# A second quarter-block product in the last map of a decoder layer: product A11·B11 of the second token block made by seven

## The chip, the cores and the metric

The kernel runs on one core of one Trainium2 chip. The metric is the device time of one execution in microseconds (us). Before the change three executions took 1734.28, 1735.79 and 1736.70 us; the median, 1735.79 us, is the time to compare with. A further execution was profiled; every time of a single instruction in this document comes from the profile.

## The reference, cut to what matters

The layer has two sub-layers. The first (an input projection, a gated convolution and a causal pooling, an output projection, a layer norm) is untouched by the change. The second is

```python
h = x * (1.0 + sc2) + sh2                       # x: 2048 tokens x 1024
f = square(relu(h @ w_mlp_in)) @ w_mlp_out      # 1024 -> 4096 -> 1024
x = layer_norm(ALPHA * x + (1.0 + g2) * f, ln2_g, ln2_b)
```

All of it is float32. The change touches `... @ w_mlp_out`, the "second map", for the second half of the tokens.

## The kernel before, in words

**Float32 by three matmuls.** Every operand of a matmul is split (`split`, L87): ScalarE (ACT) casts it to a rounded high part (L88), VectorE (DVE) subtracts that from the value (L89), which gives the low part. `mm3` (L92) multiplies high by high (L93), high by low (L94) and low by high (L95) into one PSUM bank. `tt` (L98) is every plain DVE operation on two tensors, so sums, differences and the adds from PSUM all carry line L98.

**Blocks and products.** The 2048 tokens are worked on in two blocks of 1024 (b = 0, then b = 1). In a block the second sub-layer first runs `up` for eight chunks g of 512 hidden columns, and then `down`, the second map, which multiplies the 1024 x 4096 activations A by the 4096 x 1024 weights B. A and B are cut into half blocks, A11, A12, A21, A22 and likewise B, and the product is made by seven products of half blocks or of sums of them (Winograd's form of Strassen's scheme) in place of eight. `up` makes the activation's sums and stores them in `usum`, and earlier steps made the weights' sums (`w2sum`). In `down` a product is a list of 8 chunks x 4 token tiles x 2 halves of the contraction x 3 matmuls = 192 matmuls of 128x512. `steps` gives the order of the products, each in two steps of four chunks; `table` says for each product which of two sets of four PSUM banks it uses (X or Y), whether it opens them anew, and what becomes of a bank when it is complete (`then`). The output of a block is eight tiles F[0] to F[7] of 128 tokens x 1024. Their left 512 columns are `lo_`, the right ones `hi_`. F[0..3] are the upper tokens and F[4..7] the lower ones. Products 0, 2, 4 and 6 accumulate in one set of banks X one after another; 3 and 5 share Y.

**The quarter product.** In the second block (`b in DEEPER`) product 1, A12·B21, is not made from half blocks: it enters F[0..3][:, lo_] alone, and is made by the same scheme of seven once more, over quarter blocks ("deep"). `closed` (in `up`) writes the quarter sums of A12 in `udeep`, and `sum_deep` (L974), called after some chunks of `up` as `DEEP_SUMS` says, writes those of B21 in `wdeep`. In `down` come eight sets of operands, one per chunk (`deep_operands`: two tiles of 1024 and two of 768 columns, 1.835 MB together, four casts and four subtractions), each followed by `deep_matmuls`: 7 products x 2 token tiles x 3 = 42 matmuls of 128x256. The seven products have a PSUM bank each, in the order p1, p6, p2, p7, p5, p3, p4, and stay open over all eight chunks. Then `deep_sums` puts them together in F: p1 by two ACT copies, the rest by fourteen DVE adds of 128x256, with p5 read twice. The loads of the sets hang on one another in a row (`issue_after`), three sets ahead of the matmuls; the first 12 tiles (`DIRECT`) are loaded straight into the place of their low part.

**What sets the order.** SBUF tiles come from pools: `h` (28 tiles, high and low parts), `r` (5) and `w` (6) for loads, `o` (10; eight of them are F during `down`), and eight PSUM banks `ps`. A new tile takes the place that was released first, and waits for its last reader. The instructions of each engine run in a fixed order, which comes from the order in the code and a scheduler. SP's queue issues the loads (r, w), POOL's queue the stores (usum, udeep, wdeep). At the end, `gated_first`, `last_half` and `Close` scale the output by the gate, add the residual and normalise, tile by tile.

Of the kernel before, what the change touches and what calls it, by code (L numbers as in the profile page):

```python
# [13 lines left out]
P = 128  # L14
# [20 lines left out]
DEEP_SUMS = (0,), (1,), (2,), (3,), (4, 5), (6, 7), (), ()  # L35
# [15 lines left out]
def tile_hybrid_layer(ctx: ExitStack, tc: tile.TileContext, opening, xT, x, wada, win,  # L51
# [141 lines left out]
    udeep = tc.dram_tile([NC, P, 3 * Q], F32, name="udeep")  # L193
    wdeep = tc.dram_tile([NC, P, T + 3 * Q], F32, name="wdeep")
# [779 lines left out]
    def sum_deep(g):  # L974
        a, e = t_o(T), t_o(T)
        nc.sync.dma_start(a, w2[g, 2])
# [6 lines left out]
        nc.gpsimd.dma_start(wdeep[g][:, :T], a)  # L983
        nc.gpsimd.dma_start(wdeep[g][:, T:], e[:, : 3 * Q])
# [6 lines left out]
    def up(b, g, B):  # L991
# [27 lines left out]
        save(c11, 0)  # L1019
# [19 lines left out]
        if g == 0:  # L1039
            yield  # L1040
        else:
            product(5, Z, False)
            join(c12, Z)
        s1 = t_o()
# [17 lines left out]
        def closed(s4):  # L1062
# [10 lines left out]
            nc.gpsimd.dma_start(udeep[g], e[:, : 3 * Q])  # L1073
# [42 lines left out]
    def down(b, F, g2, close):  # L1116
# [4 lines left out]
        steps = [(i, hf) for i in ((1, 0) if deeper else (0, 1)) + (2, 3, 5, 4, 6) for hf in range(2)]  # L1121
# [65 lines left out]
        def gated_first(t, ps):  # L1187
            tt(F[t + 4][:, lo_], ps, g2[:, lo_], ALU.mult)
# [19 lines left out]
        def deep_operands(g):  # L1208
            tiles = []
            for t, src, n in ((t_r, usum[g, 1], T), (lambda: t_w(F32), wdeep[g][:, :T], T),  # L1210
                              (t_r, udeep[g], 3 * Q), (lambda: t_w(F32), wdeep[g][:, T:], 3 * Q)):
                if 4 * g + len(tiles) < DIRECT:
# [6 lines left out]
                if 4 * g + len(tiles) >= DIRECT:  # L1219
                    hi, lo = t_h(), t_h()  # L1220
# [8 lines left out]
        def deep_matmuls(banks, gs, tiles, ns):  # L1229
            for n in ns:  # L1230
                (ut, uq), (wt, wq) = DEEP[n]
                if gs[0] == 0:
                    banks.append(t_ps())
                for g in gs:
                    (uh, ul), (wh, wl) = tiles[g][ut], tiles[g][wt]
                    ws_ = slice(wq * Q, wq * Q + Q)
                    for t in range(2):
                        us = slice(uq * Q + t * P, uq * Q + t * P + P)
                        mm3(banks[n][:, t * Q : t * Q + Q], uh[:, us], ul[:, us], wh[:, ws_], wl[:, ws_],
                            g == t == 0, g == NC - 1 and t == 1, True)  # L1240

        def deep_sums(banks):
            p1, p6, p2, p7, p5, p3, p4 = banks
            def both(j, k, x, ps):
                for t in range(2):
                    src = ps[:, t * Q : t * Q + Q]
                    d = F[t + 2 * j][:, QUARTERS[k]]
# [251 lines left out]
```

## Time and profile before

| | |
|---|---|
| median of three runs | 1735.79 us (1734.28 to 1736.70) |
| the profiled execution | 1735.02 us, of which its span is 1733.2 us, so 1.8 us lie outside of it |
| TensorE clock granted in it | 0.999 |
| `up` of the second block ends, the quarter product begins | 1424.06 us |
| the quarter product ends, product 0 begins | 1464.37 us |
| the last instruction ends | 1733.20 us |

How to read it: PE is TensorE, PEld its weight loads, DVE VectorE, ACT ScalarE, SP and POOL the engines whose queues issue transfers. "L95 PE" is a matmul from line 95. A row `1464.37 0.40 PE L93 ...` starts at 1464.37 us in the span and takes 0.40 us until its modelled end; matmuls overlap, so the price of one is the distance from its start to the next one's start. `[2.56 <-PE ps L95]` behind a row says that the engine had been idle for 2.56 us and that a matmul of line 95 released it. A row of the windows gives the stretch, its length, the busy time and count of instructions of PE, PEld, DVE, ACT and POOL, the clock, the busy share of the sixteen DMA engines and the GB/s. The lines themselves stand in the prediction.

### The profile page before, as it was taken

To read this page: it belongs to the slowest core of one execution; us is meant where nothing else is said; L and a number is where in the kernel's file an instruction comes from. 1 tells how busy PE (TensorE), PEld (TensorE's weight loads), DVE (VectorE), ACT (ScalarE), POOL (GpSimd) and SP (SyncE) were. 2 spreads that over 40 slices of the span, in tenths; PEclk is the share of its full clock that TensorE was granted. 3 is DMA by queue.
4 is the path that set the end of the run, shared out by engine and by line. 5 is a ranking of instruction groups with operands and counts; after the bars stand their busy time and mean duration, and the time that the engine had idled before them with its cause. 6 is when DMAs were issued, how large, how long until landed. Compare 5 with 4: busy or idle time off the path is not lost.

```text
span 1733.2 us, 21912 instructions
## 1 busy us (share of the span) xinstructions
PE 1723.5 (99%) x7855; PEld 1435.5 (83%) x7855; DVE 1314.6 (76%) x1726; ACT 868.1 (50%) x1172; POOL 205.8 (12%) x399
## 2 busy tenths in 40 slices
PE   9999999999999999999999999999999999999998
PEld 7888888888888888888888888888888889888887
DVE  8897798877777686669686789687566778665896
ACT  6323368554445554446573344775444567444451
POOL 0222220122322000100000000102111110000000
PEclk9999999999999999999999999999999999999999
DMA  9998877778888998887572366657545589777771
GB/s 387 345 337 319 302 267 269 267 262 325 311 326 319 381 418 332 291 286 284 196 271 76 110 219 219 230 185 282 215 179 222 197 290 418 294 273 249 267 264 50
DMA packets 142685, 465.24 MB, mean 268 GB/s; under 512 B 16488, under 2 KB 17008, under 8 KB 142576
## 3 DMA queue, kind: packets, MB, share of 16 engines
q1 hardware_dynamic: 97920, 303.39, 48.0%
q0 software_dynamic: 44656, 160.46, 24.4%
q8 instruction: 61, 1.00, 0.2%
q14 instruction: 48, 0.39, 0.1%
HBM read 318.55 MB, written 145.23 MB: 268 GB/s over the span
## 4 chain that ended last, share of the span: by engine, by line
PE 95%; DMA 3%; issue 1%; DVE 1%; ACT 0%; SPq 0%; POOL 0%; DVEq 0%; POOLq 0%
PE ps L95 30%; PE ps L93 30%; PE ps L94 30%; PE ps L425 3%; DMA r<-in_w 1%; DMA usum<-o 1%; PE ps L773 1%; DVE o L98 0%; DMA o<-in_w 0%; DMA o<-in_opening 0%; DVE w L89 0%; DVE r L98 0%; ACT w L88 0%; DVE o L1369 0%; SPq L108 0%
## 5 line engine op out<-in xcount | busy, mean ns | idle before, releaser
L95 PE MATMUL ps<-h,w 128*128 128x512 f32 x1312 | 510.2, 389 | 0.4 <-DVE w L89 0.4
L94 PE MATMUL ps<-h,w 128*128 128x512 f32 x1312 | 510.3, 389 | 0.0
L93 PE MATMUL ps<-h,w 128*128 128x512 f32 x1312 | 510.0, 389 | 0.0
L93 PE MATMUL ps<-h,h 128*128 128x512 f32 (+1 forms) x1176 | 444.2, 378 | 0.0
L95 PE MATMUL ps<-h,h 128*128 128x512 f32 (+1 forms) x1176 | 444.1, 378 | 0.0
L94 PE MATMUL ps<-h,h 128*128 128x512 f32 (+1 forms) x1176 | 444.0, 378 | 0.0
L88 ACT CAST h<-r 128x1024 fp32r<-128x1024 f32 (+2 forms) x186 | 187.8, 1014 | 298.0 <-PE ps L94 186.8
L95 PEld LDWEIGHTS ps<-h,w 128*128 128x128 f32 x1312 | 246.3, 188 | 52.1 <-DVE w L89 0.8
L94 PEld LDWEIGHTS ps<-h,w 128*128 128x128 f32 x1312 | 246.3, 188 | 51.5 <-DVE h L89 0.5
L93 PEld LDWEIGHTS ps<-h,w 128*128 128x128 f32 x1312 | 246.0, 188 | 51.3 <-ACT h L88 0.2
L89 DVE TENSOR_TENSOR h<-r,h 128x1024 fp32r<-128x1024 f32 (+2 forms) x186 | 217.3, 1173 | 93.5 <-ACT h L88 93.0
L88 ACT CAST w<-r 128x1024 fp32r<-128x1024 f32 x156 | 164.3, 1053 | 242.6 <-PE ps L94 231.3
L89 DVE TENSOR_TENSOR w<-r,w 128x1024 fp32r<-128x1024 f32 x156 | 190.5, 1222 | 96.3 <-ACT w L88 95.4
L94 PEld LDWEIGHTS ps<-h,h 128*128 128x128 f32 x1176 | 221.3, 188 | 41.1
L95 PEld LDWEIGHTS ps<-h,h 128*128 128x128 f32 x1176 | 221.3, 188 | 40.8
L93 PEld LDWEIGHTS ps<-h,h 128*128 128x128 f32 x1176 | 221.3, 188 | 40.5
L98 DVE TENSOR_TENSOR o<-o,o 128x1024 f32<-128x1024 f32 (+2 forms) x193 | 171.1, 890 | 41.0 <-DMA usum<-o 31.8
L98 DVE TENSOR_TENSOR o<-o,ps 128x512 f32<-128x512 f32 (+1 forms) x175 | 113.7, 658 | 54.3 <-PE ps L95 53.4
L89 DVE TENSOR_TENSOR h<-w,h 128x1024 fp32r<-128x1024 f32 x114 | 137.6, 1207 | 4.3 <-ACT h L88 4.1
L88 ACT CAST h<-w 128x1024 fp32r<-128x1024 f32 x114 | 118.6, 1040 | 12.8 <-DMA w<-wdeep 4.1
L1013 POOL DMA_DIRECT2D usum<-o x111 | 59.4, 535 | 472.3 <-ACT o L1010 195.0
L98 DVE TENSOR_TENSOR r<-r,r 128x1024 f32<-128x1024 f32 x60 | 73.4, 1223 | 21.5 <-DMA r<-in_w 17.5
(160 smaller groups left out, 1243.0 us busy)
## 6 DMA issues: line engine op xcount, KB each, us to landing
usum<-o POOLq DMA_DIRECT2D x111, 512.0 KB, 4.8
r<-usum SPq DMA_DIRECT2D x109, 512.0 KB, 5.5
w<-w2sum SPq DMA_DIRECT2D x64, 512.0 KB, 5.9
r<-in_w SPq DMA_DIRECT2D x60, 512.0 KB, 6.0
w<-in_w SPq DMA_DIRECT2D x40, 512.0 KB, 7.4
o<-in_w SPq DMA_DIRECT2D x72, 256.0 KB, 6.4
w2sum<-o POOLq DMA_DIRECT2D x64, 256.0 KB, 6.7
msum<-o POOLq DMA_DIRECT2D x18, 512.0 KB, 4.9
```

The source lines that it names most:

```text
L88: high = nc.scalar.copy(hi, src)
L89: return high.ins, nc.vector.tensor_tensor(lo, src, hi.bitcast(F32), op=ALU.subtract).ins
L93: nc.tensor.matmul(ps, whi, xhi, start=first, stop=False, skip_group_check=goes_on)
L94: nc.tensor.matmul(ps, whi, xlo, start=False, stop=False, skip_group_check=goes_on)
L95: nc.tensor.matmul(ps, wlo, xhi, start=False, stop=last, skip_group_check=goes_on)
L98: return nc.vector.tensor_tensor(out_, a, b_, op=op)
L425: nc.tensor.matmul(ps[m, h], wt[:, w : w + P], A[k][p // 2][:, hs], start=k == 0 and p == 0, stop=k == KD - 1 and p == 2)
L773: nc.tensor.transpose(ps[:, t * P : t * P + P], R[4 * h + t][:, k * P : k * P + P], ident)
L1013: nc.gpsimd.dma_start(usum[g, i], r)
```

## The change

Product 0, A11·B11, of the second block's second map is made by seven over quarter blocks too. A11·B11 enters all four quarters of the output, so its result, once put together in F[4..7][:, lo_], is added to F[0..3][:, lo_] and copied to F[0..3][:, hi_] and F[4..7][:, hi_]. What was accumulated on top of product 0 in the banks X now starts new banks, and is added to F when complete.

- `udeep` and `wdeep` have a place for each of the two products. `sum_deep` makes the weights' quarter sums of B21 (i = 1) or B11 (i = 0), and runs for both after every chunk of `up`; before, it ran eight times in all, and not after the last two chunks.
- `up` stores A11 in two pieces, makes four quarter sums of it (four DVE adds of 128x256) and stores those.
- `down` runs sixteen sets of operands back to back, eight of A12·B21 and then eight of A11·B11, and `deep_sums` twice. `DIRECT` holds for the first product's sets alone.
- Products 2 and 3 end in DVE adds to F (`add`) where ACT copies (`keep`) stood; `gated_first` takes three DVE operations for each of its four tiles where it took two.

```diff
-DEEP_SUMS = (0,), (1,), (2,), (3,), (4, 5), (6, 7), (), ()
+DEEP_SUMS = tuple(((0, g), (1, g)) for g in range(8))
...
+        if b in DEEPER:
+            e = t_o()
+            a11, a21, a12, a22 = (c11[:, i * Q : i * Q + Q] for i in range(4))
+            q1, q2, q4, q3 = (e[:, i * Q : i * Q + Q] for i in range(4))
+            tt(q1, a21, a22, ALU.add)
+            tt(q2, q1, a11, ALU.subtract)
+            tt(q3, a11, a21, ALU.subtract)
+            tt(q4, a12, q2, ALU.subtract)
+            nc.gpsimd.dma_start(usum[g, 0][:, QUARTERS[1]], q3)
+            nc.gpsimd.dma_start(udeep[0, g], e[:, : 3 * Q])
...
         def gated_first(t, ps):
-            tt(F[t + 4][:, lo_], ps, g2[:, lo_], ALU.mult)
+            add(t + 4, lo_, ps)
+            gate(t + 4, lo_)
             tt(F[t + 4][:, lo_], F[t + 4][:, lo_], rest[6][t], ALU.add)
...
-            2: (X, False, lambda t, ps: keep(t, hi_, ps)),
-            3: (Y, True, lambda t, ps: keep(t + 4, hi_, ps)),
+            2: (X, deeper, lambda t, ps: put(t, hi_, ps)),
+            3: (Y, True, lambda t, ps: put(t + 4, hi_, ps)),
...
+            work = [(i, g) for i in (1, 0) for g in range(NC)]
+            tiles = [deep_operands(*w) for w in work[:3]]
             left.pop()(t_h(F32))
...
+            for n, (i, g) in enumerate(work):
+                if n + 3 < len(work):
+                    tiles.append(deep_operands(*work[n + 3]))
+                if n + 1 == len(work):
+                    ready = operands(4)
+                if g == 0:
+                    banks = []
+                deep_matmuls(banks, g, tiles[n])
+                if g + 1 == NC:
+                    deep_sums(banks, 0 if i else 4)
+
+            for t in range(4):
+                whole = F[t + 4][:, lo_]
+                tt(F[t][:, lo_], F[t][:, lo_], whole, ALU.add)
+                nc.scalar.copy(F[t][:, hi_], whole)
+                nc.scalar.copy(F[t + 4][:, hi_], whole)
...
-        for n, (i, hf) in list(enumerate(steps))[2 if deeper else 0 :]:
+        for n, (i, hf) in list(enumerate(steps))[4 if deeper else 0 :]:
```

In instructions: PE gets 336 matmuls of 128x256 for 192 of 128x512; DVE gets 105 operations more and ACT 18; POOL's queue issues 414 transfers instead of 374, SP's 671 instead of 647.

At the seam between the two quarter products, DVE's rows in the changed kernel, from the first add of the first product's `deep_sums` on (`ps_1823` is the bank of p6, `ps_1824` p2, `ps_1825` p7; `h_1879`, `h_1882`, `h_1885` and `h_1888` are the four low parts of the ninth set, the first of A11·B11, and `h_1891`, `h_1894` belong to the tenth):

```order
L98 TENSOR_TENSOR o_1776_11468<-o_1776_11468,ps_1823_11577 128x256
L89 TENSOR_TENSOR h_1879_11886<-r_1877_11883,h_1878_11885 128x1024
L98 TENSOR_TENSOR o_1777_11469<-o_1777_11469,ps_1823_11577 128x256
L89 TENSOR_TENSOR h_1882_11892<-w_1880_11889,h_1881_11891 128x1024
L89 TENSOR_TENSOR h_1885_11898<-r_1883_11895,h_1884_11897 128x768
L89 TENSOR_TENSOR h_1888_11904<-w_1886_11901,h_1887_11903 128x768
L98 TENSOR_TENSOR o_1776_11468<-o_1776_11468,ps_1824_11584 128x256
L98 TENSOR_TENSOR o_1777_11469<-o_1777_11469,ps_1824_11584 128x256
L98 TENSOR_TENSOR o_1778_11470<-o_1776_11468,ps_1825_11591 128x256
L89 TENSOR_TENSOR h_1891_11952<-r_1889_11949,h_1890_11951 128x1024
L98 TENSOR_TENSOR o_1779_11471<-o_1777_11469,ps_1825_11591 128x256
L89 TENSOR_TENSOR h_1894_11958<-w_1892_11955,h_1893_11957 128x1024
```

DVE in the kernel before, where its one quarter product ends and product 0 begins (`ps_1799` is p6, `ps_1800` p2; the `h` are low parts of product 0's operands):

```order
L89 TENSOR_TENSOR h_1856_11836<-r_1853_11831,h_1855_11835 128x1024
L89 TENSOR_TENSOR h_1858_11840<-w_1854_11833,h_1857_11839 128x1024
L98 TENSOR_TENSOR o_1752_11332<-o_1752_11332,ps_1799_11441 128x256
L98 TENSOR_TENSOR o_1753_11333<-o_1753_11333,ps_1799_11441 128x256
L89 TENSOR_TENSOR h_1862_11848<-r_1859_11843,h_1861_11847 128x1024
L98 TENSOR_TENSOR o_1752_11332<-o_1752_11332,ps_1800_11448 128x256
```

Before, the first two low parts of what follows stood ahead of the adds; in the changed kernel every low part of the ninth set stands behind the first add. The rest of the changed sequence goes on in the same way (p5, then the bank of p3, with the low parts of the eleventh set between):

```order
L98 TENSOR_TENSOR o_1776_11468<-o_1776_11468,ps_1826_11598 128x256
L98 TENSOR_TENSOR o_1777_11469<-o_1777_11469,ps_1826_11598 128x256
L98 TENSOR_TENSOR o_1776_11468<-o_1776_11468,ps_1827_11605 128x256
L89 TENSOR_TENSOR h_1903_12018<-r_1901_12015,h_1902_12017 128x1024
L98 TENSOR_TENSOR o_1777_11469<-o_1777_11469,ps_1827_11605 128x256
L89 TENSOR_TENSOR h_1906_12024<-w_1904_12021,h_1905_12023 128x1024
```

Behind these stand two more low parts, two adds of p4 (`ps_1828`) and the second two of p5 (`ps_1826`). PE's rows in the changed kernel at the point where the second quarter product opens its sixth bank, `ps_1930` (its seven are `ps_1925` to `ps_1931`; a wait on an engine's counter stands in brackets):

```order
L94 MATMUL ps_1929_12149<-h_1894_11958,h_1896_11963 128x256
L95 MATMUL ps_1929_12149<-h_1893_11957,h_1897_11964 128x256
L93 MATMUL ps_1925_12121<-h_1905_12023,h_1902_12017 128x256 [waits Activation_49]
L93 MATMUL ps_1927_12135<-h_1905_12023,h_1902_12017 128x256
L93 MATMUL ps_1930_12156<-h_1881_11891,h_1884_11897 128x256 [waits DVE_49]
L94 MATMUL ps_1930_12156<-h_1882_11892,h_1884_11897 128x256
```

The second product's matmuls do not run set by set: the scheduler has put the ones of the banks that come free late behind those of the tenth set. `ps_1930` opens 62 rows behind the first matmul of the second product, and 64 rows of the sets nine to eleven (126 in all) stand from it on. In the first quarter product's last set, p6's last matmul stands 17 rows ahead of the end and p1's 33 rows ahead; in the kernel before, p6's last stood 30 rows ahead of the end.

78 lines of the change are left out of this document (35 added, 43 removed).

## The prediction

> **What bounds the kernel now.** I read the page's shares and the chain of work first, then the waits of PE.
>
> ```profile
> span 1733.2 us, 21912 instructions
> PE 1723.5 (99%) x7855; PEld 1435.5 (83%) x7855; DVE 1314.6 (76%) x1726; ACT 868.1 (50%) x1172; POOL 205.8 (12%) x399
> PE 95%; DMA 3%; issue 1%; DVE 1%; ACT 0%; SPq 0%; POOL 0%; DVEq 0%; POOLq 0%
> PE ps L127 <- DVE o L129: 1.1, 1, 1.1
> PE ps L425 <- DVE h L396: 0.5, 1, 0.5
> PE ps L95 <- DVE w L89: 0.4, 1, 0.4
> PE ps L127 <- DVE h L200: 0.4, 1, 0.4
> ```
>
> PE is busy for 99% of the span and holds 95% of the chain that ended last. Its waits for other engines come to 2.4 us in the whole run (1.1 + 0.5 + 0.4 + 0.4). So the time is the sum of the matmuls, and a change can win only what it takes from that sum, and lose whatever makes PE wait where it doesn't now. The windows of the second map show how near the other resources stand to that:
>
> ```profile
> 1424.06:1464.37 40.31, 40.31 (x338) 40.31 (x336) 33.30 (x37) 27.63 (x32) 2.67 (x5) 1.00 1.02 408
> 1445.00:1465.00 20.00, 20.00 (x166) 19.91 (x166) 16.52 (x19) 15.07 (x18) 0.00 (x0) 1.00 1.03 418
> 1425.00:1430.00 5.00, 5.00 (x44) 5.00 (x43) 4.75 (x7) 5.00 (x7) 0.69 (x3) 1.00 0.98 352
> 1464.37:1733.20 268.83, 261.62 (x1178) 217.49 (x1176) 193.04 (x237) 111.60 (x149) 4.27 (x8) 1.00 0.66 239
> ```
>
> The quarter product (first row) is the tightest stage of the kernel: PE without a gap for 40.31 us, DVE at 33.30 of 40.31 us (83%), weight loads as long as the stage, and the DMA engines full at 408 GB/s. What follows it (last row) runs at 239 GB/s and DVE at 72%. The change puts a second stage of the tight kind in the place of an easy one.
>
> **What PE saves.** The matmuls are priced by the distance of their starts.
>
> ```profile
> 1464.25 0.28 PE L95 MATMUL ps<-h,h 128*128 128x256 f32 x1
> 1464.37 0.40 PE L93 MATMUL ps<-h,h 128*128 128x512 f32 x1
> 1465.76 0.39 PE L93 MATMUL ps<-h,h 128*128 128x512 f32 x1
> 1467.80 0.39 PE L93 MATMUL ps<-h,h 128*128 128x512 f32 x1
> ```
>
> Nine matmuls of 128x512 lie between 1465.76 and 1467.80: 2.04 / 9 = 0.2267 us each, so product 0 by half blocks is 192 x 0.2267 = 43.5 us. A quarter product is 40.31 us for 336 of 128x256, or 0.120 each. The saving is 43.5 - 40.3 = **3.2 us**, and no other term of the change can make PE faster. The narrow form costs 53% of the wide one and not half, which takes two thirds of what one product in eight would be. The Trainium skill prices them alike: "TensorE: Matmul & The Clock Gate", section "Back-to-back issue gap", gives 262 cycles for 256 columns and 518 for 512; worked out from these as an estimate at its 2.4 GHz, the saving would be 4.8 us, but the trace has 0.120 and 0.2267 us, and its rows decide.
>
> **Up.** Each of the eight chunks gets four DVE adds of 128x256 (0.34 us each by the row of seven below, some 1.4 us), and the weights' sums for one more chunk.
>
> ```profile
> 1355.15 1.23 DVE L98 TENSOR_TENSOR o<-o,o 128x1024 f32<-128x1024 f32 x1 [3.10 <-DMA usum<-o]
> 1370.72 1.23 DVE L89 TENSOR_TENSOR w<-r,w 128x1024 fp32r<-128x1024 f32 x1 [4.22 <-ACT w L88]
> wdeep<-o POOLq DMA_DIRECT2D x8, 512.0 KB, 6.2
> wdeep<-o POOLq DMA_DIRECT2D x8, 384.0 KB, 6.0
> udeep<-o POOLq DMA_DIRECT2D x8, 384.0 KB, 5.7
> ```
>
> These rows lie in the sixth chunk of `up`, which makes two sums of weights already, and DVE idles 3.1 and 4.2 us at single places of it while PE waits for nothing. I cost the DVE work of `up` at 0; that idle time hides it, and without it 1.4 us a chunk would show.
>
> **The start of the quarter product.** The stores are another matter at the last chunk. Both sums of the eighth chunk are now made there, where before the last two chunks made none: 2 x (512 + 384) KB = 1.835 MB more, just ahead of a stage whose DMA engines are full. At 417 to 418 GB/s (the second row of the windows above) that is 4.4 us by which the loads come later. What stands against it is the lead of the sets:
>
> ```profile
> 1445.87 0.96 DVE L89 TENSOR_TENSOR h<-w,h 128x768 fp32r<-128x768 f32 x1
> 1450.54 0.95 DVE L89 TENSOR_TENSOR h<-w,h 128x768 fp32r<-128x768 f32 x1
> ```
>
> These are the last low parts of the sixth and seventh set, ready at 1446.8 and 1451.5. A set takes PE 40.31 / 8 = 5.04 us, so the sixth begins at 1424.06 + 5 x 5.04 = 1449.26, and its second product, the first that reads that part, 0.7 us later at 1450.0. The lead is 3.2 us, and 3.5 for the seventh. A delay of 4.4 us against 3.2 leaves **1.0 us** of stall (1.2, rounded down since some of the stores land ahead of the loads). Its bounds are 0, if all of them do, and 2 us, if DVE's order makes the late loads push its own work back further.
>
> **The seam.** Here the second product's operands meet the first one's `deep_sums`. E is the end of the first product. Its prices:
>
> ```profile
> 1460.25 0.65 ACT L1249 COPY o<-ps 128x256 f32<-128x256 f32 x2 [3.05 <-PE ps L95]
> 1460.78 1.06 ACT L88 CAST h<-r 128x1024 fp32r<-128x1024 f32 x1
> 1461.74 1.05 ACT L88 CAST h<-w 128x1024 fp32r<-128x1024 f32 x1
> 1449.67 0.95 DVE L89 TENSOR_TENSOR h<-r,h 128x768 fp32r<-128x768 f32 x1
> 1461.03 0.75 DVE L98 TENSOR_TENSOR o<-o,ps 128x256 f32<-128x256 f32 x2 [2.56 <-PE ps L95]
> 1461.88 1.23 DVE L89 TENSOR_TENSOR h<-r,h 128x1024 fp32r<-128x1024 f32 x1
> 1463.02 0.41 DVE L98 TENSOR_TENSOR o<-o,ps 128x256 f32<-128x256 f32 x1
> 1470.36 2.40 DVE L98 TENSOR_TENSOR o<-o,ps 128x256 f32<-128x256 f32 x7
> ```
>
> By distances of starts, a low part of 1024 columns is 1.14 us of DVE (1461.88 to 1463.02), one of 768 columns 0.86 (1449.67 to 1450.54, above), an add 0.33 ((2.40 - 0.41) / 6). In the kernel before p6's bank was complete 30 matmuls ahead of the end, at 1464.37 - 3.6 = 1460.77, and the add began 0.26 us later. Now it is complete 17 matmuls ahead, at E - 2.0, so DVE begins at E - 1.8. It then has its rows in the order shown: p6 (two adds), four low parts of the ninth set, p2 (2), p7 (2) and p5 (2) among four low parts of the tenth, p3 (2) among the eleventh's, and at the end p4 and p5. Summed up: the ninth set is ready at E + 2.9, p2's bank free at 3.6, p7's at 5.4, the tenth set at 8.3, p5's first adds at 8.9, p3's bank at 10.7, the eleventh set at 13.6, p4's bank at 14.3, p5's at 14.9. ACT isn't late: its casts at 0.95 us run ahead of all of these.
>
> PE has 126 matmuls in the ninth to eleventh set, 15.1 us. Its first low part comes at E + 1.2, but the waits that it meets one after another overlap, and the last one decides: the sixth bank, opened behind 62 matmuls (at E + 7.4 if nothing held it up), with 64 behind it. Banks are taken in the order of their release, so I take it for p3's, free at 10.7. PE ends the eleventh set at 10.7 + 64 x 0.12 = E + 18.4 instead of 15.1: **3.3 us** of stall. Bounds: if DVE's adds slip in earlier, or the bank is p7's, what is left is the first wait of 1.2 us; if the bank is p5's, read last, 14.9 + 7.7 - 15.1 = 7.5 us. The value taken is that of the order of the adds. What is queued behind PE's waiting matmul is the rest of the three sets, and DVE, which waits for none of it there, goes on.
>
> **The end of the second product.** The low parts of product 2's first operands now stand behind the add of p6 as well; by the same count their weights' part is ready at 1.2 us after the end, of which the first matmuls of 0.2267 us cover some: **0.5 us** (0 to 1.2). The four adds and eight copies that spread the result have until product 2's banks are added, at least a step of 96 matmuls or 21.8 us later, and cost nothing.
>
> **The tail.** Two rows price the four adds more in `gated_first`, and one the adds of product 3.
>
> ```profile
> 1704.68 0.69 DVE L98 TENSOR_TENSOR o<-o,r 128x512 f32<-128x512 f32 x1
> 1709.40 0.69 DVE L98 TENSOR_TENSOR o<-o,ps 128x512 f32<-128x512 f32 x1 [4.02 <-PE ps L95]
> 1593.92 1.23 DVE L98 TENSOR_TENSOR r<-r,o 128x1024 f32<-128x1024 f32 x1 [10.58 <-DMA r<-nsave]
> ```
>
> Four adds of 0.69 us are 2.8 us, and DVE idles 4.0 us behind the last of these operations: 0. Products 2 and 3 now need DVE where ACT did the copies. At product 3's end an add of the last bank can come to stand behind an operation that waits for the residual's load (third row, 10.58 us idle); PE opens that bank again for product 5's last tile, 18 matmuls or 4.1 us later. Bounds 0 and 6.5 us (10.6 - 4.1), taken 0, since a wait of which all lies behind that product's end would need the load to be issued 10 us later than now.
>
> **The sum.** -3.2 + 1.0 + 3.3 + 0.5 = +1.6 us on the profiled execution's 1735.02 us: 1736.6. The median stands 0.8 us over that execution, so the forecast is **1737.5 us**, rounded up.
>
> **Rivals.**
> 1. *The waits are hidden and only the saving shows.* For it: two of the three stalls are 1 us or less, and PE waits nowhere in this stretch now. Against it: at the seam DVE has 14.9 + 1.8 = 16.7 us of work in an unbroken row, and PE must have its middle. Time: 1735.8 - 3.2 = 1732.6.
> 2. *Slower: the sixth bank is p5's.* It is read twice, by DVE's last two adds at E + 14.9. Then the stall at the seam is 7.5 us instead of 3.3 and the time 1737.5 + 4.2 = 1741.7. For it: p5's bank is read first ahead of p3's. Against it: PE's row that opens the sixth bank waits for DVE, and the next wait for DVE, 12 rows on, is for the eleventh set's second low part (E + 11.9), which would need no wait if DVE were already known to be at 14.9. This decides from the place of the bank alone.
> 3. *Slower: the transfers bind at the start.* In the window from 1425 to 1430 they ran at 352 GB/s. If that held from the start of the stage to the sixth set, 25 us, 0.065 x 25 = 1.6 MB would be missing on top of the 1.835 MB, 8 us at 417 to 418 GB/s: less the lead of 3.2, a stall of 4.9 instead of 1.0 us, so 1741.4. Against it: 408 GB/s over the whole stage. The Trainium skill, "DMA: Bandwidth & Descriptors", section "Where 436 GB/s comes from", speaks for this rival: between HBM and SBUF a core's share of the memory, about 358 GB/s, binds. The trace disagrees with that as a limit, with 418 GB/s over 20 us.
> 4. *Slower: product 3's add waits for the residual*: up to 6.5 us, 1744.0; it decides only if DVE reaches that row before the load lands and after product 3 has ended.
>
> **How the numbers follow.** The forecast has 0.52, the first rival 0.13, the second 0.15, the third 0.12, the fourth 0.08. The forecast's own terms reach from -3.2 + 0 + 1.2 + 0 = -2.0 to -3.2 + 2 + 3.3 + 1.2 = +3.3 without the second rival's bank, or 1733.8 to 1739.1, a little more with the runs' own spread of 1.2 us on either side. The range of 8 in 10 is 1732.3 to 1742.5: it takes in the first three rivals. A measurement can tell 0.2% from no change here, 3.5 us; the saving alone is 3.2. So faster by more has 0.04 (part of the first rival); within 0.2%, 1732.3 to 1739.3, are the rest of the first rival (0.09), the forecast without its upper end (0.44) and a little of the fourth (0.03), 0.56 together; slower are the rest of the forecast (0.08) and of the fourth (0.05), the second and the third: 0.40.
>
> **What would show it.** Each quarter product at 0.120 us a matmul, and a list of PE's waits with new rows for DVE's L98 and L89, in the 15 us behind the first product's end, of 3 to 4 us together; about 1 us in the sixth and seventh set for a load; half a microsecond behind the second product. If the seam shows no wait, the first rival holds and my row of DVE is wrong; if it shows 7 us, the bank is p5's. If `up` ends later than 1424 us, its cover was thinner than I took it for. If waits lie behind 1600 us, it is the fourth rival or the tail, which I cost at nothing.

## The result and the profile after

The changed kernel takes 1738.36 us (median of 14 runs, 1737.30 to 1739.48). The kernel before, run beside it, takes 1734.59 us (14 runs, 1734.16 to 1736.70), 1.2 us less than the three runs that the prediction started from. The ratio is 1.0019, with an interval of 1.0011 to 1.0027: slower by 3.8 us. The forecast was 1737.5 us, 1.7 us more than before; of the change it gave less than half, and that the time is only 0.9 us off it is luck in part, since the kernel before took 1.2 us less beside it. The profiled execution took 1738.62 us, and its span grew by 3.6 us, from 1733.2 to 1736.8.

The page's shares, the chain of work, and then the waits of PE in the whole run:

```profile
span 1736.8 us, 22481 instructions
PE 1723.7 (99%) x7999; PEld 1441.0 (83%) x7999; DVE 1360.5 (78%) x1832; ACT 880.2 (51%) x1190; POOL 227.2 (13%) x439
PE 97%; DMA 1%; DVE 1%; issue 1%; ACT 0%; DVEq 0%; SPq 0%; ACTq 0%
```

```profile
PE ps L94 <- DVE h L89: 1.4, 2, 1.0
PE ps L93 <- ACT o L1000: 1.4, 1, 1.4
PE ps L127 <- DVE o L129: 1.1, 1, 1.1
PE ps L93 <- DVE o L98: 1.0, 2, 0.6
PE ps L93 <- ACT h L88: 0.6, 1, 0.6
PE ps L425 <- DVE h L396: 0.2, 1, 0.2
```

The list has four new rows: waits for low parts (L89), for adds (L98), for a cast (L88), and one for an ACT copy of L1000, which is `keep` in `up`. Where they lie shows PE's timeline:

```profile
1180.44 0.50 PE L93 MATMUL ps<-h,w 128*128 128x512 f32 x1 [1.39 <-ACT o L1000]
...
1425.48 0.28 PE L93 MATMUL ps<-h,h 128*128 128x256 f32 x1
...
1451.68 0.50 PE L93 MATMUL ps<-h,h 128*128 128x256 f32 x2 [0.61 <-ACT h L88]
...
1466.91 0.28 PE L93 MATMUL ps<-h,h 128*128 128x256 f32 x1
1468.21 0.39 PE L94 MATMUL ps<-h,h 128*128 128x256 f32 x1 [1.01 <-DVE h L89]
...
1472.40 0.39 PE L93 MATMUL ps<-h,h 128*128 128x256 f32 x1 [0.58 <-DVE o L98]
...
1477.73 0.39 PE L93 MATMUL ps<-h,h 128*128 128x256 f32 x1 [0.47 <-DVE o L98]
...
1510.70 0.86 PE L93 MATMUL ps<-h,h 128*128 128x512 f32 x3
1511.99 0.50 PE L94 MATMUL ps<-h,h 128*128 128x512 f32 x1 [0.43 <-DVE h L89]
...
1729.28 0.28 PE L95 MATMUL ps<-h,h 128*128 128x256 f32 x1
```

The time of each term is the distance between such places, not the idle time in brackets, since the first matmuls behind a wait are slower too. `up` ends at 1425.48 instead of 1424.06: +1.4. (The profile of before has a wait of 0.43 us at 519 us, in the first block, which this one hasn't, so the wait in `up` itself costs somewhat more than 1.4.) The first quarter product takes 1466.91 - 1425.48 = 41.4 us instead of 40.3: +1.1. The second takes 1510.70 - 1466.91 = 43.8 us: +3.5 over 40.3. In the kernel before, product 0 ended by its price at 1464.37 + 43.53 = 1507.90, and the last matmul, at 1725.71, stood 217.8 us behind that; here it stands 1729.28 - 1510.70 = 218.6 us behind the second product: +0.8. Less the saving of 43.5 - 40.3 = 3.2 us, that is 1.4 + 1.1 + 3.5 + 0.8 - 3.2 = 3.6 us, the growth of the span. The windows over both quarter products show 82.47 us of PE work in 85.22, and the transfers at 393 GB/s:

```profile
1425.48:1510.70 85.22, 82.47 (x673) 81.06 (x672) 70.13 (x88) 55.73 (x65) 4.84 (x9) 1.00 1.00 393
```

### The profile page after: what moved, and what is told of

It is laid out like the page before. It is cut to its first block, busy times and chain, and to the rows that moved or that the text cites. A ratio compares the mean times of both kernels' runs of the same rounds, so it can differ in the third digit from the quotient of the medians.

```text
span 1736.8 us, 22481 instructions
## 1 busy us (share of the span) xinstructions
PE 1723.7 (99%) x7999; PEld 1441.0 (83%) x7999; DVE 1360.5 (78%) x1832; ACT 880.2 (51%) x1190; POOL 227.2 (13%) x439
## 4 chain that ended last, share of the span: by engine, by line
PE 97%; DMA 1%; DVE 1%; issue 1%; ACT 0%; DVEq 0%; SPq 0%; ACTq 0%
PE ps L94 31%; PE ps L93 31%; PE ps L95 31%; PE ps L425 3%; PE ps L773 1%; DMA r<-udeep 1%; DMA w<-w2sum 0%; DVE h L89 0%; DVE o L98 0%; PE ps L149 0%; DVE h L200 0%; PE ps L127 0%; ACT h L88 0%; DVE o L1391 0%; DVE o L1397 0%
## 5 line engine op out<-in xcount | busy, mean ns | idle before, releaser
L88 ACT CAST h<-r 128x1024 fp32r<-128x1024 f32 (+1 forms) x194 | 194.4, 1007 | 275.7 <-PE ps L94 150.5
L88 ACT CAST w<-r 128x1024 fp32r<-128x1024 f32 x156 | 164.2, 1053 | 244.8 <-PE ps L94 232.5
L89 DVE TENSOR_TENSOR h<-r,h 128x1024 fp32r<-128x1024 f32 (+1 forms) x194 | 224.3, 1161 | 75.7 <-ACT h L88 75.2
L94 PEld LDWEIGHTS ps<-h,h 128*128 128x128 f32 x1224 | 230.2, 188 | 41.0 <-DVE h L89 2.6
L93 PEld LDWEIGHTS ps<-h,h 128*128 128x128 f32 x1224 | 228.2, 188 | 41.2 <-DVE o L98 1.5
L95 PEld LDWEIGHTS ps<-h,h 128*128 128x128 f32 x1224 | 230.2, 188 | 38.0
L89 DVE TENSOR_TENSOR w<-r,w 128x1024 fp32r<-128x1024 f32 x156 | 190.2, 1220 | 81.2 <-ACT w L88 80.2
L98 DVE TENSOR_TENSOR o<-o,o 128x1024 f32<-128x1024 f32 (+2 forms) x221 | 183.1, 834 | 43.2 <-DMA usum<-o 34.2
L98 DVE TENSOR_TENSOR o<-o,ps 128x512 f32<-128x512 f32 (+1 forms) x197 | 124.1, 640 | 63.4 <-PE ps L95 53.2
L89 DVE TENSOR_TENSOR h<-w,h 128x1024 fp32r<-128x1024 f32 x122 | 144.8, 1187 | 4.1 <-ACT h L88 4.0
L88 ACT CAST h<-w 128x1024 fp32r<-128x1024 f32 x122 | 125.2, 1026 | 16.2 <-DMA w<-wdeep 7.6
L1013 POOL DMA_DIRECT2D usum<-o x103 | 55.1, 535 | 378.0 <-DVE o L98 166.3
L98 DVE TENSOR_TENSOR r<-r,r 128x1024 f32<-128x1024 f32 x60 | 73.3, 1222 | 24.8 <-DMA r<-in_w 20.3
```

Of the source, the lines that this page charges most:

```text
L88: high = nc.scalar.copy(hi, src)
L89: return high.ins, nc.vector.tensor_tensor(lo, src, hi.bitcast(F32), op=ALU.subtract).ins
L93: nc.tensor.matmul(ps, whi, xhi, start=first, stop=False, skip_group_check=goes_on)
L94: nc.tensor.matmul(ps, whi, xlo, start=False, stop=False, skip_group_check=goes_on)
L95: nc.tensor.matmul(ps, wlo, xhi, start=False, stop=last, skip_group_check=goes_on)
L98: return nc.vector.tensor_tensor(out_, a, b_, op=op)
```

## The experiments

All ratios are to the kernel before on the same chip. "Both quarter products" is the distance from the first matmul of 128x256 to the first one behind the second product; without any wait it would be 2 x 40.31 = 80.6 us. It and the end of `up` are read from each run's one profiled execution. Those of up_only and seam_copies took 2.0 and 2.2 us more than their medians, with waits of PE of 0.93 us at 519 us and of 1.78 us at 1400 us, so their `up` ends later than in most executions. Differences of 1 to 2 us between the variants are within the overlap of the intervals; there the distances in the traces are the firmer evidence.

| run | median, us | ratio (interval) | over before, us | `up` ends | both quarter products, us |
|---|---|---|---|---|---|
| changed kernel | 1738.36 | 1.0019 (1.0011 to 1.0027) | +3.8 | 1425.48 | 85.22 |
| up_only | 1737.35 | 1.0017 (1.0008 to 1.0026) | +2.8 | 1426.86 | 41.14 (one) |
| down_only | 1732.20 | 0.9986 (0.9977 to 0.9996) | -2.4 | 1423.26 | 81.02 |
| seam_copies | 1736.49 | 1.0013 (1.0004 to 1.0022) | +1.9 | 1426.94 | 83.88 |
| sums_spread | 1756.26 | 1.0123 (1.0108 to 1.0139) | +21.7 | 1444.54 | 83.62 |
| e_only | 1733.68 | 0.9993 (0.9984 to 1.0002) | -1.1 | 1424.93 | 81.02 |
| w_only | 1737.67 | 1.0015 (1.0006 to 1.0024) | +2.9 | 1425.31 | 84.10 |
| last_no_adds | 1737.43 | 1.0015 (1.0007 to 1.0024) | +2.7 | 1425.22 | 84.20 |
| sums_in_block1 | 1743.10 | 1.0045 (1.0033 to 1.0058) | +8.4 | 1434.07 | 81.03 |
| seam_order | 1737.46 | 1.0018 (1.0009 to 1.0028) | +2.7 | 1425.25 | 84.69 |
| seam_p3_first | 1737.07 | 1.0013 (1.0005 to 1.0022) | +2.4 | 1425.45 | 83.57 |
| best | 1734.85 | 1.0001 (0.9992 to 1.0010) | +0.1 | 1423.74 | 83.78 |
| best_act | 1732.26 | 0.9987 (0.9978 to 0.9996) | -2.4 | 1423.43 | 81.03 |

### up_only: the change's `up` without the second quarter product

The kernel before with the changed kernel's lines in `up` and `sum_deep`; product 0 reads all of `usum[g, 0]`, so A11 is stored whole and q3 goes to a place of its own:

```diff
+            nc.gpsimd.dma_start(qdeep[g], q3)
+            nc.gpsimd.dma_start(udeep[0, g], e[:, : 3 * Q])
```

> The kernel before, with the stage `up` of the changed kernel: all sums for the second quarter product are made and stored, but product 0 stays one of half blocks and reads none of them. My theory (the work of `up` is not hidden): PE waits 1.4 us at the beginning of the second chunk, near 1180 us, and about 1.1 us in the sixth or seventh set of the quarter product, so 2.5 us over the kernel before, and a seam as before. Rival (the wait at 1180 us was an accident of one execution): nothing at 1180 us, at most 1.1 us over the kernel before.

PE's rows at the second chunk and in the sixth set:

```profile
1181.82 0.50 PE L93 MATMUL ps<-h,w 128*128 128x512 f32 x1 [1.39 <-ACT o L1001]
...
1453.03 0.39 PE L93 MATMUL ps<-h,h 128*128 128x256 f32 x1 [0.58 <-ACT h L88]
```

Both are there, the first with the same 1.39 us, and the median grew by 2.8 us: `up` is not hidden. The theory missed one thing. The end of the one quarter product waits as well, 0.43 us for a low part at 1469.29, which the kernel before does not: something in `up` reaches into a later stage.

### down_only: the second map's change with the `up` of before

```diff
-DEEP_SUMS = tuple(((0, g), (1, g)) for g in range(8))
+DEEP_SUMS = ((1, 0),), ((1, 1),), ((1, 2),), ((1, 3),), ((1, 4), (1, 5)), ((1, 6), (1, 7)), (), ()
...
-            for t, src, n in ((t_r, usum[g, i], T), (lambda: t_w(F32), wdeep[i, g][:, :T], T),
+            for t, src, n in ((t_r, usum[g, i], T), (lambda: t_w(F32), wdeep[1, g][:, :T], T),
```

> The changed kernel with the stage `up` of the kernel before: the second quarter product reads the operands of the first once more, so that A11·B11 is replaced by other data of the same size. My theory (three terms of the second map, without the late stores): -3.2 of matmuls, +3.5 at the seam, +0.8 behind the second product, so +1.1 us over the kernel before, with no wait in the first product's sets. Rival (the loads of sixteen sets in a row are too much for the DMA engines by themselves): the wait of about 1.1 us in the sixth or seventh set is still there, +2.2 us.

Expected was +1.1, measured -2.4 us. The windows over both quarter products, with PE's busy time behind the length:

```profile
1423.26:1504.28 81.02, 81.02 (x673) 80.77 (x672) 66.64 (x80) 53.92 (x64) 2.66 (x5) 1.00 0.99 385
```

81.02 us, and PE busy in all of it: the seam costs 0.4 us, not 3.5. The sums of the first product, the operands of the second and PE's matmuls are the same in number as in the changed kernel. So the seam's price isn't that of two quarter products behind one another. It comes from `up`, and the effects don't add: +2.8 and -2.4 make +0.4, and the whole change +3.8.

### seam_copies: the late banks given back early

```diff
+            k, j4 = t_o(), t_o()
+            for d, bank in ((k[:, :H], p5), (k[:, H:], p3), (j4[:, :H], p4)):
+                nc.scalar.copy(d, bank)
+            p5, p3, p4 = k[:, :H], k[:, H:], j4[:, :H]
```

> The changed kernel, but the banks of p5, p3 and p4 are copied to SBUF by ACT as soon as they are complete, and DVE adds from there. My theory (the seam waits for PSUM banks that DVE gives back too late): the last bank is free 5 to 6 us behind the end of the first product instead of 14, and the seam's 3.5 us fall to about 1.5, what the ninth set's low parts cost; 2.0 us under the changed kernel. Rival (DVE's work as a whole is too much at the seam, wherever the banks are): the seam stays at 3 us or more, since no add is saved, and the time is the changed kernel's.

1.9 us under the changed kernel. Both products take 83.9 us, of which 0.8 belong to the wait in the sixth set (0.53 us of idle time there; the second product begins at 1468.04, 41.1 us behind the first), so the seam costs about 2.5 us instead of 3.5. PE's waits that are left at the seam:

```profile
1469.33 0.38 PE L94 MATMUL ps<-h,h 128*128 128x256 f32 x1 [1.01 <-DVE h L89]
...
1473.52 0.39 PE L93 MATMUL ps<-h,h 128*128 128x256 f32 x1 [0.58 <-DVE o L98]
```

The wait at the sixth bank is gone, and the one for the ninth set's first low part is as long as before. PE does wait for banks at the seam, behind something that is late already.

### sums_spread: other chunks for the weights' sums

```diff
-DEEP_SUMS = tuple(((0, g), (1, g)) for g in range(8))
+DEEP_SUMS = (((0, 0),), ((1, 0), (0, 1)), ((1, 1), (0, 2)), ((1, 2), (0, 3), (1, 3)), ((0, 4), (1, 4), (0, 5)), ((1, 5), (0, 6), (1, 6)), ((0, 7), (1, 7)), ())
```

> The changed kernel with the weights' sums in other chunks of `up`: 1, 2, 2, 3, 3, 3, 2 and 0 of them instead of 2 each. My theory (the sums in the first chunk make the wait at 1180 us, those in the last chunk the late loads): both waits go, 2.5 us under the changed kernel. Rival A (the wait at 1180 us comes of the four new adds and their tile, not of the weights' sums): only 1.1 us go. Rival B (three sums in a chunk are too many): new waits in the middle of `up`, no gain.

Rival B, far beyond what it said: 21.7 us slower. In the sixth to eighth chunk PE waits 2.2, 3.6 and 6.0 us for the low parts of `up`'s own weights, and behind each wait it runs at half its clock. The first of them in the windows, right behind the wait (the clock stands behind the five engines):

```profile
1325.77:1327.04 1.27, 1.27 (x6) 1.05 (x6) 1.20 (x4) 0.00 (x0) 0.29 (x2) 1.00 1.01 348
1327.04:1330.41 3.37, 3.37 (x9) 2.63 (x8) 2.25 (x4) 0.00 (x0) 1.39 (x3) 0.50 0.98 325
1330.41:1334.50 4.09, 4.09 (x19) 3.41 (x18) 0.90 (x3) 0.00 (x0) 0.00 (x0) 0.99 1.02 396
```

The wait at 1180 us is still there with one sum after the first chunk, so it isn't a matter of the second sum alone.

### e_only and w_only: the two halves of `up`

e_only keeps A11's quarter sums and has the weights' sums of before; w_only has both weights' sums after every chunk and leaves A11's out. The second product reads the first one's operand for what is missing (lines not shown):

```diff
 e_only:
-DEEP_SUMS = tuple(((0, g), (1, g)) for g in range(8))
+DEEP_SUMS = ((1, 0),), ((1, 1),), ((1, 2),), ((1, 3),), ((1, 4), (1, 5)), ((1, 6), (1, 7)), (), ()
 w_only:
-        if b in DEEPER:
-            e = t_o()
...
-            nc.gpsimd.dma_start(udeep[0, g], e[:, : 3 * Q])
```

> The changed kernel with the weights' sums of the kernel before (B21 alone, none after the last two chunks); A11's quarter sums are made and stored, and the second quarter product multiplies them by B21's sums, so that A11·B11 is replaced by A11·B21. Theory after the first runs (what costs at the start and at the seam is the weights' sums of the last chunks, which set where DVE's low parts of the ninth set stand): no wait in the first product's sets, a seam of 0.4 us as with the stage `up` of before, and only the 1.4 us at 1180 us, since A11's tile in the first chunk puts ACT's copies behind a third cast: 1.0 us under the kernel before. Rival (A11's sums and their stores are enough to bring the waits back): start and seam of 4 us or more in all, 3 us over the kernel before.

> The other half: the changed kernel with both weights' sums after every chunk, but without A11's quarter sums; the second quarter product multiplies the first one's activations by B11's sums, so that A11·B11 is replaced by A12·B11. The same theory: the seam's 3.5 us, the 1.1 us at the start and 0.8 us behind the second product are back, and at 1180 us ACT's copies stand behind a third cast here too, 1.4 us: about the time of the changed kernel, 3 to 4 us over the kernel before. Rival: the weights' sums are hidden, and it stays 2 us under the kernel before.

Both came out as the theory had it: -1.1 us and +2.9 us. e_only has both quarter products in 81.02 us and a single new wait:

```profile
1180.00 0.50 PE L93 MATMUL ps<-h,w 128*128 128x512 f32 x1 [1.39 <-ACT o L1000]
```

w_only has the seam (84.10 us for both products) and the same 1.4 us at the second chunk. So either half is enough for the wait at 1180 us, and the weights' sums alone make the seam. In w_only the sixth set does not wait.

### last_no_adds: the last chunk's bytes without its adds

```diff
-        a, e = t_o(T), t_o(T)
+        a = t_o(T)
...
+        e = t_o(T) if g < NC - 1 else a
...
+        if g == NC - 1:
+            nc.gpsimd.dma_start(wdeep[i, g][:, :T], a)
+            nc.gpsimd.dma_start(wdeep[i, g][:, T:], a[:, : 3 * Q])
+            return
```

> The changed kernel, but after the last chunk the weights are stored as they are, the same number of bytes without the eight adds, so that one eighth of both quarter products' weights is wrong. Theory of the prediction (the bytes of these stores delay the loads): the wait of about 1.1 us in the sixth or seventh set stays, and with it the changed kernel's time. Rival, from the trace (eight adds of 0.34 us stand ahead of the fourth set's low parts on DVE and keep its r and w tiles, and the next loads wait for them): the wait falls to 0.3 us or less; DVE's order at the seam is unchanged and so is its 3.5 us; 1 us under the changed kernel.

0.9 us under the changed kernel, the rival's number, and no wait in the sixth set. As a proof of that wait's cause it is weak: seam_p3_first below, with the changed kernel's `up` and first product untouched, has none either, while the changed kernel, seam_copies and seam_order show 0.61, 0.53 and 0.29 us. The wait comes and goes by small amounts. Firm is what the adds do to the loads. The load of the sixth set's third tile goes out, in the kernel before, in this run and in the changed kernel:

```profile
1432.29 0.32 SPq L1218 DMA_DIRECT2D r<-udeep  x1
```

```profile
1434.40 0.32 SPq L1240 DMA_DIRECT2D r<-udeep  x1
```

```profile
1437.47 0.32 SPq L1235 DMA_DIRECT2D r<-udeep  x1
```

From the beginning of the quarter product (1424.06, 1425.22, 1425.48) that is 8.2, 9.2 and 12.0 us. The eight adds cost 2.8 of the 3.8 us, at the same bytes. They stand on DVE ahead of the low parts of the first sets, whose `r` tiles the next loads need.

Two sets later it is the bytes, not the adds. SP's wait for a store between 1436 and 1456 us, and the load behind it, the first of the eighth set, in the changed kernel, in this run and in e_only:

```profile
SPq L1235 <- DMA usum<-o: 8.6, 1, 8.6
1452.04 0.32 SPq L1235 DMA_DIRECT2D r<-usum  x1
```

```profile
SPq L1240 <- DMA usum<-o: 9.6, 1, 9.6
1451.85 0.32 SPq L1240 DMA_DIRECT2D r<-usum  x1
```

```profile
SPq L1235 <- DMA usum<-o: 3.0, 1, 3.0
1441.71 0.32 SPq L1235 DMA_DIRECT2D r<-usum  x1
```

The load reads the last chunk's part of A12, and POOL's queue has the store of that behind the last chunk's weights' sums. With their bytes and without their adds the wait is as long as in the changed kernel; without the sums (e_only) it is 3.0 us, and the load goes out 10 us earlier. The ninth set's loads follow it in the row, so they are late as well.

### sums_in_block1: six of the weights' sums moved ahead

```diff
-DEEP_SUMS = tuple(((0, g), (1, g)) for g in range(8))
+DEEP_SUMS = ((((1, 0), (0, 0)), ((1, 1),), (), (), (), (), (), ((0, 1), (1, 2), (0, 2))), ((), ((1, 3), (0, 3)), ((1, 4), (0, 4)), ((1, 5), (0, 5)), ((1, 6), (0, 6)), ((1, 7), (0, 7)), (), ()))
...
-            if b in DEEPER:
-                for i, n in DEEP_SUMS[g]:
-                    sum_deep(i, n)
+            for i, n in DEEP_SUMS[b][g]:
+                sum_deep(i, n)
```

> The changed kernel, correct in all its parts, with six of the sixteen weights' sums made in the first block's `up` (2, 1, 0, 0, 0, 0, 0, 3 after its chunks) and ten in the second's (0, 2, 2, 2, 2, 2, 0, 0), none after the first chunk and none after the last two. Theory: none of the waits at 1180 us, at the start and at the seam is left, and the saving shows: 2 to 2.5 us under the kernel before. Rival (the sums cost wherever they are; three sums of the first block's last chunk hold up its own second map): a new wait of 1 to 3 us at the beginning of the first block's second map, and a time between the kernel before and the changed one.

The waits at 1180 us, at the start and at the seam are gone, all three, as the theory said (81.03 us for both products). One new one costs more than all of them; it lies not where the rival had it but behind the first block's first chunk, where two sums were put on top of what is made there:

```profile
340.56 0.80 PE L93 MATMUL ps<-h,w 128*128 128x512 f32 x1 [7.42 <-ACT o L1000]
```

### seam_order: DVE's order pinned

```diff
-                split(r[:, :n], hi[:, :n], lo[:, :n])
+                lows.append(split(r[:, :n], hi[:, :n], lo[:, :n])[1])
...
+            with nullcontext() if t0 else tc.issue_after(lows[4 * NC + 1]):
+                both(0, 1, (0, 0), p6)
```

> The changed kernel with one thing pinned: the first product's adds of p6 may not stand ahead of the low part of the ninth set's second tile, so that DVE has at the seam the order that it has without the weights' sums of the last chunks; no work is taken away. Theory (the seam's 3.5 us are the price of an order, in which the ninth set stands behind the adds and all the later banks behind it): the seam falls to 0.4 to 1 us, and the waits at 1180 us and in the sixth set stay; 2.5 to 3.1 us under the changed kernel. Rival (the ninth set's data come too late, and the order only follows them): DVE waits for them ahead of the adds, PE's banks come later still, and the time is the changed kernel's or more.

Missed; the rival had it. The ninth set's first low parts now stood ahead of the adds, but DVE waited 1.70 us for ACT's cast ahead of the first of them, and the second product, from 1466.11 to 1509.94, took 43.8 us as in the changed kernel. The 0.9 us by which the median fell are what the shorter wait in the sixth set and the missing one behind the second product come to. So the theory that DVE's order makes the seam is wrong as it stood.

### seam_p3_first: p3's adds ahead of p5's

```diff
-            both(0, 1, (0, 1), p5)
             both(0, 1, (0, 1), p3)
+            both(0, 1, (0, 1), p5)
```

> The changed kernel with p3's two adds ahead of p5's first two in the order of the sums. Theory (at the seam PE waits for p3's bank, with half of three sets queued behind it): the bank is free at 8.9 us behind the end of the first product in place of 10.7, PE's rows behind it are 71 in place of 64, and the seam costs 2.3 to 2.5 us in place of 3.5; about 1 us under the changed kernel. Rival (it is p5's bank, as the prediction's second rival had it): it is read later than before, and the seam is not shorter.

Half of it: the two products take 83.57 us, and without a wait in the sixth set that leaves 3.0 us for the seam instead of 3.5. The rest of the 1.3 us in the median is the missing wait of that set. The bank is p3's, but with it earlier the low parts come next and hold PE nearly as long.

### best: the sums where none had cost, and DVE's order pinned

The lines of seam_order, and:

```diff
-DEEP_SUMS = tuple(((0, g), (1, g)) for g in range(8))
+DEEP_SUMS = (((), ((1, 0),), (), (), (), (), (), ((0, 0), (1, 1), (0, 1))), ((), ((1, 2), (0, 2)), ((1, 3), (0, 3)), ((1, 4), (0, 4)), ((1, 5), (0, 5)), ((1, 6), (0, 6)), ((1, 7), (0, 7)), ()))
```

> The changed kernel, correct in all its parts, with the order at the seam pinned as in the run before, and the weights' sums at places where none of the waits arose so far: 0, 1, 0, 0, 0, 0, 0, 3 after the first block's chunks and 0, 2, 2, 2, 2, 2, 2, 0 after the second's. Theory: the saving of 3.2 us less 0.4 at the seam and 0.4 behind the second product, 2.4 us under the kernel before, and no wait of PE behind the first 10 us. Rival (each place that is filled costs its own wait, the sums cost 1 to 3 us wherever they are put): no faster than the kernel before.

The waits in `up` and in the sixth set are gone, the seam of 3.2 us is not, and the time is that of the kernel before. This run shows why. ACT and then DVE ahead of the seam:

```profile
1454.12 0.83 ACT L88 CAST h<-w 128x768 fp32r<-128x768 f32 x1
1459.93 0.65 ACT L1264 COPY o<-ps 128x256 f32<-128x256 f32 x2 [4.98 <-PE ps L95]
1460.46 1.06 ACT L88 CAST h<-r 128x1024 fp32r<-128x1024 f32 x1
```

```profile
1461.56 1.23 DVE L89 TENSOR_TENSOR h<-r,h 128x1024 fp32r<-128x1024 f32 x1 [5.31 <-ACT h L88]
```

ACT idles 4.98 us ahead of the two copies of p1, because p1's bank is complete only then, and the ninth set's first cast stands behind the copies. DVE idles 5.31 us for that cast. In the traces of down_only, e_only and sums_in_block1 the order on ACT is the other one: two casts of the ninth set, then the copies.

### best_act: ACT's copies of p1 behind two casts

best, with one pin more (`parts` holds each cast and its low part):

```diff
+            with nullcontext() if t0 else tc.issue_after(parts[4 * NC + 1][0]):
+                both(0, 0, None, p1)
```

> The last run's kernel with one more thing pinned: ACT's two copies of p1 may not stand ahead of the cast of the ninth set's second tile. The last two runs took the first theory of the seam down: with DVE's rows in the good order the seam still cost 3.1 to 3.2 us, and DVE idled 5.3 us ahead of the ninth set's first low part. New theory: it is ACT's order. The two copies wait for p1's bank, which PE completes 4 us ahead of the end of the first product, and the ninth set's casts stand behind them though their data are there; the low parts, and all that DVE does at the seam, come 4 us late. With the copies behind two casts the seam falls from 3.1 to about 0.4 us, and the time is 2.7 us under the last run's, 2.5 us under the kernel before. Rival (the loads of the ninth set come too late): ACT waits for them where it waited for PE, the seam stays at 2 to 3 us, and the time at the kernel before's.

The seam is gone: 81.03 us for both products, and 2.6 us less than best from the place of two copies of 0.3 us each. ACT at the same place, and all waits of PE in the run:

```profile
1454.79 1.05 ACT L88 CAST h<-r 128x1024 fp32r<-128x1024 f32 x1 [0.38 <-DMA r<-usum]
1456.03 1.05 ACT L88 CAST h<-w 128x1024 fp32r<-128x1024 f32 x1 [0.20 <-DMA w<-wdeep]
1459.63 0.37 ACT L1264 COPY o<-ps 128x256 f32<-128x256 f32 x1 [2.55 <-PE ps L95]
```

```profile
PE ps L127 <- DVE o L129: 1.1, 1, 1.1
PE ps L127 <- DVE h L200: 0.6, 1, 0.6
PE ps L425 <- DVE h L396: 0.2, 1, 0.2
```

No wait is left behind the first 9 us. The second quarter product is then worth 2.4 us (0.9978 to 0.9996): the saving of 3.2 less 0.4 at the seam and 0.4 behind.

## Why the prediction was right, and where it was not

**The bound and the saving** hold. PE's busy time is 1723.7 us in 1736.8, and the two quarter products take 81.0 us in the four kernels without the waits, so 3.2 us less 0.4 of the seam are what the matmuls give. The Trainium skill's prices ("TensorE: Matmul & The Clock Gate", section "Back-to-back issue gap") would have made it 4.8; here 81.02 us for 672 matmuls are 0.1206 each, and the trace disagrees.

**`up` was the step that failed**: costed at 0 because DVE idles there, and 1.4 us in fact, or 1.7 from down_only to e_only (1423.26 to 1424.93), between which PE has no other wait behind the first 9 us. The cover that the prediction named was DVE's; the wait is for ACT. ACT at the beginning of the second chunk, before and in the changed kernel:

```profile
1174.74 1.07 ACT L1000 COPY o<-ps 128x512 f32<-128x512 f32 x2
1176.73 0.59 ACT L1000 COPY o<-ps 128x512 f32<-128x512 f32 x1 [0.93 <-PE ps L95]
1179.45 0.59 ACT L1000 COPY o<-ps 128x512 f32<-128x512 f32 x1 [2.13 <-PE ps L95]
1179.94 1.05 ACT L88 CAST w<-r 128x1024 fp32r<-128x1024 f32 x1
```

```profile
1178.86 1.04 ACT L88 CAST w<-r 128x1024 fp32r<-128x1024 f32 x1 [3.36 <-PE ps L94]
1179.81 2.04 ACT L1000 COPY o<-ps 128x512 f32<-128x512 f32 x4
```

Before, `keep`'s four copies stand ahead of a cast; now they stand behind one, which waits for PE to free a `w` tile, and so they do in up_only, e_only and w_only. With no weights' sum after the first chunk (sums_in_block1, best) they do not all stand behind it, and PE does not wait. What an added row moves on the engines beside it was in the order of ACT, which the prediction did not look at.

**The start** was forecast at 1.0 and measured at 1.1 us, for a reason that was wrong in part. For the sixth set it is mostly not the 1.8 MB of late stores; with the same bytes and without the adds its load goes out 2.8 us earlier. The stores do hold the loads up, but from the eighth set on (last_no_adds above), where the prediction did not look for them. The wait is marginal, 0 to 0.6 us of idle time between runs with the same code ahead of it.

**The seam** was forecast at 3.3 and measured at 3.5 us, and the steps that were named are there. The add of p6 begins and the add that frees p3's bank ends here:

```profile
1465.13 0.42 DVE L98 TENSOR_TENSOR o<-o,ps 128x256 f32<-128x256 f32 x1 [2.20 <-ACT h L88]
...
1477.27 0.41 DVE L98 TENSOR_TENSOR o<-o,ps 128x256 f32<-128x256 f32 x1
```

With E at 1466.91, p6's add begins at E - 1.8 (forecast E - 1.8), the first low part releases PE at E + 1.3 (1.2), and PE opens the sixth bank at E + 10.8, 0.05 us behind the second add of p3 (10.7). So it is p3's bank and the second rival is out. What the prediction did not see is that this chain hangs on one row: ACT's copies of p1 ahead of the ninth set's casts. In best, where the data are there in time, putting them behind two casts takes the seam from 3.2 to 0.4 us. In the changed kernel itself the ninth set's data are late as well, 8 to 9 us behind loads issued near 1454, so there both reasons hold DVE up; that would explain why seam_order, which removed neither, gained nothing. The copies moved with the late data left as they are was not tried, so how the 3.5 us divide between the two is open. The close number is luck in part: "ACT isn't late" was wrong, and DVE's order, which the sum was built on, is not enough to make the seam or to remove it (3.5 us in seam_order and 3.2 in best with the low parts ahead). ACT's first cast ended at 1464.75, about when p6's bank was complete (E - 2.0 by the prediction's count), so DVE's row began when the prediction said, for two reasons at once of which it saw one.

**Behind the second product** 0.8 us for 0.5, and **the tail** 0 as forecast: no wait of PE behind 1512 us, so the fourth rival is out. **The third** is out too: in the first 25 us, where it had 352 GB/s, the changed kernel moved 406, and over both products 393. The Trainium skill's share of the memory for one core, about 358 GB/s ("DMA: Bandwidth & Descriptors", section "Where 436 GB/s comes from"), is no limit in this run either. **The first rival**, that only the saving shows, needed another order of rows and other places for the sums. A side remark of the prediction is off: the narrow form leaves 3.2 of the 5.4 us that one product in eight would be (43.5 / 8), so it takes two fifths and not two thirds.

In all, by the distances in the two profiles, every term but that of `up` came within 0.3 us, and the 2.0 us between the sum (+1.6) and the growth of the span (+3.6) are 1.4 of `up` and 0.1, 0.2 and 0.3 of the start, the seam and the place behind the second product.

## What to carry to other kernels

Where a chain of tightly fed stages has one engine at 99%, read the order of every helper engine at each seam, the one with the short work above all: two copies of 0.3 us that wait for PE cost 2.6 us by what stood behind them. A stage that looks covered by idle time on one engine can still move rows on another, so an addition there should be compared with the kernel before on all engines, and its effect looked for in the stages behind it, down to the load that must wait for the last store. Test the halves of a change by themselves: here they came to +2.8 and -2.4 us, the whole to +3.8, and the difference was the fault.

## What the runs showed of the hardware that was not expected

An idle time of 2.19 us on PE in the middle of a run was enough to lose half its clock. The granted clock fell to 0.50 for 3.37 us, 1.3 us behind the end of that wait (sums_spread, the windows above), and matmuls of 128x512 came at 0.43 us instead of 0.227. The waits of 1.39 us at the second chunk, in nine of the runs, and one of 1.78 us in seam_copies are followed by matmuls at full speed. Half the clock for 3.37 us loses 1.7 us, so a wait of 2.2 us costs 3.9; in sums_spread waits of 11.8 us (three) and 1.1 us, with three times 1.7 us, are 18 of the 19.1 us by which `up` is longer than in the changed kernel (1444.54 against 1425.48). The Trainium skill ("TensorE: Matmul & The Clock Gate", section "What's actually happening") gives about 3.4 us both for the idle time that halves the clock and for the busy time that restores it: the 3.37 us agree with the second, the 2.19 us do not with the first.
